# Buffers of split weights kept as the last weight ring, and a rearranged router start, in a one-core hybrid decoder step

## The chip, the cores and the metric

The kernel runs on one core of a Trainium2 chip. The metric is the time of one execution on the device, in microseconds; lower is better. Times of the kernel before are the median of 3 runs. TensorE is called PE here, VectorE DVE, ScalarE ACT, GpSimd POOL; SP is the engine that issues most of the DMA transfers.

## What is computed

One layer of a decoder for 256 prompt tokens and 32 sample tokens (8 sequences of 4), 288 tokens in all, with a model width of 1024, in fp32:

```python
xn = rms_norm(x)
q_sb, k_sb, v_sb, q_m, k_m, v_m, gate_sb, gate_m = split(xn @ w_in)       # 1024 x 5120
m = sigmoid(gate_sb) * (stick_breaking(q_sb, k_sb, v_sb) @ w_proj_sb) \
  + sigmoid(gate_m) * (block_attention(q_m, k_m, v_m) @ w_proj_moba)
x = x + m @ w_out
x = x + hier_moe(rms_norm(x))    # best of 4 groups, then 2 of its 4 experts; 16 SwiGLU experts of 256
y = rms_norm(x) * g_final
```

The sample tokens also attend to 256 past keys each, which are gathered from paged pools. Outputs are y and the new keys and values. On the inputs used, the 288 tokens choose 576 experts; 234 of these choices fall on experts 10 to 15, and no expert has more than 64 tokens.

## The kernel before, in words

Activations lie transposed, features on partitions, tokens along the free axis. The work goes through these stages.

**Projections and attention (0 to 217 us).** `w_in` is loaded in chunks of 256 columns (1 MB, tag `raw`, three buffers). Each group of 128 columns (`g1`) is split into a high part h (a cast on ACT, L355) and a low part l (a subtraction on DVE, L360), and `held` (L374, L375, L378) makes three products of it: 16 matmuls that use h, then 8 that use l. h and l have three buffers each (tags `wh` and `wl` of the pool `wp`). Attention runs between those groups. The order on PE is set by a hand-written driver; on ACT and DVE a scheduler sets it from its own model of the program.

**Output projections (217 to 274 us).** `proj` and `outp` do the same with `w_proj` and `w_out`; the last three groups, o5, o6 and o7, hold the last three buffers of h and l. The router's logits (`lgp`) are accumulated beside them.

**Router (274 to 289 us).** ACT and DVE follow the written order from here. `natural` turns x back to token rows, `rows_out` stores them to `x2_d` in DRAM. DVE finds groups and experts and makes one-hot tables; PE counts the places in each expert (`cums`), then makes, for the 8 pairs of experts, the list of tokens of each slot (`index_mm`: token numbers times one-hot, L995; `index` adds the parts on DVE). A pair has 128 slots. Pair 0 does not use its list: its rows are selected by a product with the one-hot table (`pick`, L1013, in two halves of 512 columns, the copies out of PSUM on ACT for half 0 and on DVE for half 1, L1014). Its norm factors come from another such product (L1053 into `pi`, copied to `rsl` by L1063). `turn_xe` (L1022) then transposes the rows and scales them (L1024). `warm` (L201) is a matmul of ones whose result nobody reads; one stands before `cums`, one behind. Pairs 1 to 7 are gathered from `x2_d` by an indirect DMA on POOL's queue (`fetch`, L1004), which leaves out slots whose index is past the end.

**Experts (289 to 397 us).** `up` (L1185) multiplies a pair with gate and up weights, `down` (L1233) with the down weights. In the middle of pair 0, `late_router` counts again for an overflow check (L1081) and makes the other lists. Results of pairs 0 to 4 are stored as rows to `y_d` (L1244), and six indirect DMAs (`gathered`, L1282) later fetch two rows for each token; `rows2` holds the row numbers and `add_rows` (L1291) adds the rows with the weights `w2`. A choice that falls on a late expert (10 to 15, pairs 5 to 7, added by products instead) points to one of 16 rows of zeros behind the others, written by L917.

**The weight ring.** The 48 MB of expert weights come as 48 parts of 1 MB (two DMAs for gate and up, one for down), in order of use. They rotate through 19 slots that are set up as memory comes free: `RINGS = (8, 5, 3, 3)`. The third group are the `raw` buffers. The fourth are three slots of a new pool, `ring3`, allocated after `wp` has been released. SP issues the parts in order; a part waits until all products that used its slot are done. Parts are counted from 0 here: parts 16, 17 and 18 are the first of the fourth group, and part 19 is the first that takes a slot already used, that of part 0, which pair 0 has read when four of its eight steps k are done.

```python
    ring_loads(RINGS[2])                 # L896: parts 13 to 15, right after the last outp
    gx.release()
    wp.release()
    for c in range(2):                   # L927
        for t in range(c == 0, 3):
            natural(t, c)
        if c:
            ring_loads(1)                # part 16
        last = rows_out(slice(c * 512, c * 516 + 512))
    with tc.issue_after(last.ins):
        ring_loads(RINGS[3] - 1)         # parts 17 and 18
```

Of the kernel before, what the change touches and what calls it, by code (L numbers as in the profile page):

```python
# [7 lines left out]
F32 = mybir.dt.float32  # L8
# [111 lines left out]
def build(tc, I, O):  # L120
# [17 lines left out]
    x2_d = dr.tile([NT, D + 4], F32, name="x2_d")  # L138
    y_d = dr.tile([NONE + 16, D], F32, name="y_d")
    NBUF = {"mm": 2, "at": 4, "ss": 1, "po": 1}  # L140
# [64 lines left out]
    def startup():  # L205
# [51 lines left out]

        hl = [[wp.tile([128, 8, 128], F32R, tag=f"w{c}", name=f"{c}i{4 + j}") for c in "hl"] for j in range(2)]

# [80 lines left out]

    splits, first = {}, []

# [10 lines left out]
    def split_h(src, name, shape=(8, 128)):  # L353
        h = wp.tile([128, *shape], F32R, tag="wh", name=f"h{name}")
        nc.scalar.copy(h, src)  # L355
        return h

    def split_l(src, h, name, shape=(8, 128)):
        l = wp.tile([128, *shape], F32R, tag="wl", name=f"l{name}")
        V.tensor_sub(l, src, h.bitcast(F32))  # L360
        return l
# [533 lines left out]
    drv.run()  # L895
    ring_loads(RINGS[2])  # L896
    gx.release()
    wp.release()


    wk = tc.alloc_tile_pool(name="wk", bufs=1)
    rings.append(tc.alloc_tile_pool(name="ring3", bufs=RINGS[3], side="right"))
    mo = tc.alloc_tile_pool(name="mo", bufs=1)
# [11 lines left out]
    for i in range(2):  # L915
        nc.gpsimd.memset(xes[i], 0.0)
    nc.gpsimd.dma_start(y_d[NONE:, :], xes[0][0:16, 0:D])  # L917
    ioi = mo.tile([128, 384], I32, tag="PT", name="ioi", bufs=2)
# [8 lines left out]
    for c in range(2):  # L927
        for t in range(c == 0, 3):
            natural(t, c)
        if c:  # L930
            ring_loads(1)
        last = rows_out(slice(c * 512, c * 516 + 512))
    with tc.issue_after(last.ins):
        ring_loads(RINGS[3] - 1)
    for t in range(3):
# [23 lines left out]

    warm(1, 416)  # L960
    cums = P("mm", "cums")
# [47 lines left out]
    def pick(c):  # L1009
        po = P("at", f"xe0{c}")  # L1010
        cs = slice(c * 512, c * 512 + 512)
        for t in range(3):
            mm(po, slots_of(t, 0), x2[:TW[t], t, cs], start=(t == 0), stop=(t == 2))  # L1013
        (nc.scalar.copy, V.tensor_copy)[c](xe0[:, cs], po)  # L1014

# [35 lines left out]
    V.tensor_tensor(ee, ee, bc(s4[:, :, None], 2), op=ALU.mult)  # L1051
    for t in range(3):
        mm(pi[:, 16:17], slots_of(t, 0), x2[:TW[t], t, D:D + 1], start=(t == 0), stop=(t == 2))  # L1053
    xe0 = gt.tile([128, 4 * NT], F32, tag="xT", name="xe0")
    pick(0)
    index_mm(0, 3)
    index(0, 3)
    fetch(1)
    fetch(2)
    pick(1)  # L1060
    xeTs[0] = gt.tile([128, 4 * NT], F32, tag="xT", name="xeT0")[:, 0:D].rearrange("p (k t) -> p k t", k=8)
    rsl[0] = mo.tile([128, 1], F32, tag="rsl", name="rsl0", bufs=3)
    V.tensor_copy(rsl[0], pi[:, 16:17])  # L1063
    turn_xe(xeTs[0], xe0, 0)
    V.tensor_reduce(es, ee, axis=AX.X, op=ALU.add)
# [13 lines left out]
    def late_router():  # L1079
        for t in range(3):  # L1080
            mm(cums[:, 48:64], onesb[:TW[t], :], OHs[:TW[t], t, :], start=(t == 0), stop=(t == 2))  # L1081
        index_mm(3, 8)
        index(3, 8)
        V.tensor_reduce(mxc, cums[:, 48:64], axis=AX.X, op=ALU.max)
        V.tensor_copy(mxi, mxc)
        V.tensor_scalar(tmp, posm, float(CAP) + 0.5, None, op0=ALU.is_ge)
        V.tensor_mul(cw, cw, tmp)
        token_rows()
        hold.__exit__(None, None, None)

    def token_rows():

        pk, row, ok = s3("pk", 2), s3("row", 2), s3("ok", 2)
        for i in range(2):
            V.tensor_mul(tmp, posm, OH[i])
            V.tensor_reduce(pk[:, :, i], tmp, axis=AX.X, op=ALU.add)
        V.scalar_tensor_tensor(row, ei[:, :, 0:2], float(CAP), pk, op0=ALU.mult, op1=ALU.add)
        V.tensor_scalar(ok, pk, CAP + 0.5, None, op0=ALU.is_lt)
        V.scalar_tensor_tensor(ok, ei[:, :, 0:2], 2 * LATE - 0.5, ok, op0=ALU.is_lt, op1=ALU.mult)
        V.scalar_tensor_tensor(row, row, -(NONE + 1.0), ok, op0=ALU.add, op1=ALU.mult)  # L1100
        V.tensor_scalar(rows2, row, float(NONE), None, op0=ALU.add)

# [172 lines left out]
    def gathered():  # L1275

        last.append(tc.manual_schedule(engines={mybir.EngineType.Activation, mybir.EngineType.DVE}))
        last[0].__enter__()
        g = [ring_slot(48 + t, f"yg{t}") for t in range(3)]
        for t in (1, 0, 2):  # L1280
            for i in range(2):
                nc.gpsimd.indirect_dma_start(out=g[t][:TW[t], i * D:(i + 1) * D], out_offset=None, in_=y_d[:, :],  # L1282
                                             in_offset=bass.IndirectOffsetOnAxis(ap=rows2[:TW[t], t, i:i + 1], axis=0),
                                             bounds_check=NONE + 15, oob_is_err=False)
        yg.extend(g)
        yield 0.0, 0.0
# [111 lines left out]
```

## Time and profile before

| | |
|---|---|
| median of 3 runs | 411.39 us (411.09 to 413.56) |
| profiled execution | 411.19 us |
| its span, first to last instruction | 409.3 us |
| PE busy | 391.2 us (96%) |
| DVE, ACT, POOL busy | 205.5, 182.9, 92.8 us |
| DMA | 111.04 MB, mean 271 GB/s |
| mean granted TensorE clock | 0.995 |

A timeline row gives start, length, engine, line, operation, output and inputs, shape and count; a bracket at its end is the idle time of the engine before it and what ended it. The end of a matmul is modelled, so a row's length runs over the start of the next; here the distance of two starts is used for what an instruction costs on PE. SPq is SP's DMA queue. "x_d" is `x2_d`, "xe" on L1013 is the picked rows, "inv" is `pi`, "gu" is the result of `up` and "pd" that of `down`.

### The profile page before, as it was taken

Reading aid. Unit: us, or ns where it says so; the run is one execution under the profiler, and the core shown is the slowest. Engines: PE = TensorE matmul, PEld = TensorE weight load, DVE = VectorE, ACT = ScalarE, POOL = GpSimd, SP = SyncE. Lnnn points to the kernel's source line nnn. Section 1 sums busy time; section 2 is a strip of 40 time slices with the busy share of each in tenths; the row PEclk is TensorE's granted clock in tenths of the full one; section 3 lists DMA queues with packets and bytes.
Section 4 is the critical chain, followed back from the end, with each engine's and each line's share of the span. In section 5 each row is a group of like instructions: output and inputs, shape, how many; then the busy total and the mean of one; then the engine's idle time right before and its main releaser. Section 6 shows DMA issues by size and latency. Waiting matters only on the chain.

```text
span 409.3 us, 7097 instructions
## 1 busy us (share of the span) xinstructions
PE 391.2 (96%) x2690; PEld 293.0 (72%) x2690; DVE 205.5 (50%) x436; ACT 182.9 (45%) x361; POOL 92.8 (23%) x128
## 2 busy tenths in 40 slices
PE   7999999998999999999999999999899999999990
PEld 4999988867987987897999999994443333333350
DVE  3784468556633647133646794324640111126874
ACT  4864357667753665665544445223001111112353
POOL 2540221204352330510100142330102222023011
PEclk9999999999999999999999999999999999999997
DMA  8999736736733973673699999929799999999903
GB/s 260 320 335 295 234 106 219 236 104 217 260 111 106 336 281 104 205 258 104 168 371 412 325 356 364 420 95 286 254 306 417 409 412 423 414 417 410 353 24 123
DMA packets 56969, 111.04 MB, mean 271 GB/s; under 512 B 7653, under 2 KB 36845, under 8 KB 54881
## 3 DMA queue, kind: packets, MB, share of 16 engines
q1 hardware_dynamic: 49648, 86.55, 59.1%
q0 software_dynamic: 7120, 23.95, 16.1%
q8 instruction: 23, 0.38, 0.4%
q14 instruction: 18, 0.14, 0.1%
q10 hardware_dynamic: 160, 0.03, 0.0%
HBM read 104.64 MB, written 7.43 MB: 274 GB/s over the span
## 4 chain that ended last, share of the span: by engine, by line
PE 71%; DMA 18%; DVE 4%; ACT 2%; issue 2%; POOL 0%; DVEq 0%; SPq 0%; POOLq 0%; ACTq 0%
DMA w<-in_w_expert_up 15%; PE g L378 9%; PE g L374 9%; PE g L375 9%; DMA w<-in_w_expert_down 4%; PE gu L1185 4%; PE pk L643 3%; PE p L374 2%; PE p L375 2%; PE p L378 2%; PE ss L649 2%; PE pos L674 2%; PE pd L1233 2%; PE g L302 2%; PE o L374 2%
## 5 line engine op out<-in xcount | busy, mean ns | idle before, releaser
L374 PE MATMUL g<-xTh,hi 128*128 128x288 f32 x304 | 88.4, 311 | 0.0
L375 PE MATMUL g<-xTl,hi 128*128 128x288 f32 x304 | 83.3, 296 | 0.0
L1185 PE MATMUL gu<-w,xeT 128*64 128x512 f32 x256 | 60.3, 598 | 0.8 <-DMA w<-in_w_expert_up 0.5
L374 PEld LDWEIGHTS g<-xTh,hi 128*128 128x128 f32 x304 | 57.2, 188 | 0.9 <-issue 0.7
L375 PEld LDWEIGHTS g<-xTl,hi 128*128 128x128 f32 x304 | 57.4, 189 | 0.0
L378 PE MATMUL g<-xTh,li 128*128 128x288 f32 x304 | 49.3, 300 | 0.0
L360 DVE TENSOR_TENSOR li<-rawi,hi 128x1024 fp32r<-128x1024 f32 x38 | 46.1, 1215 | 4.7 <-ACT hi L355 4.7
L355 ACT CAST hi<-rawi 128x1024 fp32r<-128x1024 f32 x38 | 39.7, 1048 | 15.6 <-PE g L375 15.4
L378 PEld LDWEIGHTS g<-xTh,li 128*128 128x128 f32 x304 | 42.8, 189 | 1.7 <-issue 1.7
L1185 PEld LDWEIGHTS gu<-w,xeT 128*64 128x64 f32 x256 | 18.1, 136 | 31.8 <-issue 29.7
L1233 PE MATMUL pd<-w,hT 128*64 128x512 f32 x128 | 29.2, 598 | 0.0
L1024 DVE TENSOR_TENSOR xeT<-xe,gpk 128x512 f32<-128x512 f32 x16 | 10.4, 686 | 22.9 <-PE xe L1022 22.9
L532 DVE TENSOR_TENSOR gate<-g,rb 128x288 f32<-128x288 f32 x16 | 7.3, 456 | 28.7 <-PE g L378 28.7
L644 ACT COPY KT<-pk 128x512 f32<-128x512 f32 x29 | 18.0, 642 | 7.2 <-PE pk L643 6.7
L1203 DVE SCALAR_TENSOR_TENSOR h<-gu,rsl,h 128x256 f32<-128x256 f32 x8 | 3.9, 484 | 34.4 <-ACT h L1200 34.3
L1200 ACT ACTIVATE h<-gu,rsl 128x256 f32<-128x256 f32 x8 | 3.8, 474 | 35.9 <-PE gu L1185 19.8
L1004 POOL DMA_INDIRECT xe<-x_d,inv x7 | 7.3, 1037 | 55.0 <-DVE rsl L1172 26.2
L1233 PEld LDWEIGHTS pd<-w,hT 128*64 128x64 f32 x128 | 8.6, 136 | 15.4 <-issue 13.7
L643 PE MATMUL pk<-blob,kp 128*128 128x128 f32 x128 | 19.4, 274 | 0.1
L374 PE MATMUL p<-oTh,hp 128*128 128x288 f32 x64 | 17.5, 296 | 0.0
L375 PE MATMUL p<-oTl,hp 128*128 128x288 f32 x64 | 17.4, 294 | 0.0
L1243 ACT COPY y<-pd 128x512 f32<-128x512 f32 x10 | 5.9, 586 | 23.6 <-PE pd L1233 23.6
(306 smaller groups left out, 719.3 us busy)
## 6 DMA issues: line engine op xcount, KB each, us to landing
rawi<-in_w_in SPq DMA_DIRECT2D x19, 1024.0 KB
w<-in_w_expert_gate SPq DMA_DIRECT2D x32, 512.0 KB
w<-in_w_expert_up SPq DMA_DIRECT2D x32, 512.0 KB
w<-in_w_expert_down SPq DMA_DIRECT2D x16, 1024.0 KB
rawo<-in_w_out SPq DMA_DIRECT2D x4, 1024.0 KB
y_d<-y POOLq DMA_DIRECT2D x10, 256.0 KB
rawp<-in_w_proj_sb SPq DMA_DIRECT2D x2, 1024.0 KB
rawp<-in_w_proj_moba SPq DMA_DIRECT2D x2, 1024.0 KB
```

What stands on the lines that cost most here:

```text
L302: mm(o[j], hl[j][a][:, k, :], b[:, k, :], start=(k == 0 and a == 0 and b is xTh), stop=(k == 7 and a == 1))
L355: nc.scalar.copy(h, src)
L360: V.tensor_sub(l, src, h.bitcast(F32))
L374: mm(o, h[:, k, :], mh[k], start=(k == 0), stop=False)
L375: mm(o, h[:, k, :], ml[k], start=False, stop=False)
L378: mm(o, l[:, k, :], mh[k], start=False, stop=(k == n - 1))
L643: nc.tensor.transpose(pv[:, j, :], kp[:, c, j * 128:(j + 1) * 128], ident)
L644: nc.any.tensor_copy(kt[:, :, c:256:2], pv)
L649: mm(pt[32 * bb:32 * bb + 32, 0:260], Qb[:, j, 4 * G + bb, :, :].rearrange("p h q -> p (h q)"), KT[bb][:, j, :], start=(j == 0), stop=(j = ...
L1024: i = V.tensor_mul(xeT[:, ks, :], pv, gpk[:, ks, None].broadcast_to([128, 4, 128]))
L1185: mm(pt[64 * i:64 * i + 64, :], xeTs[pr][:, k, 64 * i:64 * i + 64], W[pr, k // 4, i][:, :, k % 4, :], start=(k == 0), stop=(k == 7))
L1233: mm(pd[64 * i:64 * i + 64, :], hT[:, k, 64 * i:64 * i + 64], W[pr, 2, i][:, k, c * 512:(c + 1) * 512], start=(k == 0), stop=(k == 1))
```

## The change

- **Split weights.** h and l of a group now are the two halves of one tile (tag `w`, 8 KB a partition, three buffers), so both come free together, after the last product with l. The same memory as before.
- **Last ring.** The pool of these tiles is not released; it is the fourth group of the ring. Parts 16 to 18 are issued right behind 13 to 15, each when its buffer comes free, ahead of the row stores.
- **Rows of late experts.** The zero rows and their store are gone. Such choices get a row number past the end, which the gather leaves out; their weight in `w2` is set to 0 by one more DVE multiplication.
- **Router.** The first `warm` is two matmuls instead of one. Pair 0 has no list made. Its norm product stands behind the second half of `pick` rather than ahead of the first. The copy of the second half is shared by ACT and DVE, 256 columns each. The count for the overflow check stands right ahead of pair 0's `up` rather than inside it, and the copy to `rsl` stands behind `turn_xe`.

```diff
-    y_d = dr.tile([NONE + 16, D], F32, name="y_d")
+    y_d = dr.tile([NONE, D], F32, name="y_d")
...
     def split_h(src, name, shape=(8, 128)):
-        h = wp.tile([128, *shape], F32R, tag="wh", name=f"h{name}")
+        hl = wp.tile([128, 2, *shape], F32R, tag="w", name=f"hl{name}")
+        h = hl[:, 0]
+        lows[name] = hl[:, 1]
...
     def split_l(src, h, name, shape=(8, 128)):
-        l = wp.tile([128, *shape], F32R, tag="wl", name=f"l{name}")
+        l = lows.pop(name)
...
-    ring_loads(RINGS[2])
+    rings.append(wp)
+    ring_loads(RINGS[2] + RINGS[3])
     gx.release()
-    wp.release()
...
-    rings.append(tc.alloc_tile_pool(name="ring3", bufs=RINGS[3], side="right"))
...
-    nc.gpsimd.dma_start(y_d[NONE:, :], xes[0][0:16, 0:D])
...
-        if c:
-            ring_loads(1)
-        last = rows_out(slice(c * 512, c * 516 + 512))
-    with tc.issue_after(last.ins):
-        ring_loads(RINGS[3] - 1)
+        rows_out(slice(c * 512, c * 516 + 512))
...
-    warm(1, 416)
+    warm(2, 416)
...
-        (nc.scalar.copy, V.tensor_copy)[c](xe0[:, cs], po)
+        if c == 0:
+            nc.scalar.copy(xe0[:, cs], po)
+        else:
+            nc.scalar.copy(xe0[:, 512:768], po[:, 0:256])
+            V.tensor_copy(xe0[:, 768:1024], po[:, 256:512])
...
-    for t in range(3):
-        mm(pi[:, 16:17], slots_of(t, 0), x2[:TW[t], t, D:D + 1], start=(t == 0), stop=(t == 2))
...
-    index_mm(0, 3)
-    index(0, 3)
+    index_mm(1, 3)
+    index(1, 3)
...
     pick(1)
+    for t in range(3):
+        mm(pi[:, 16:17], slots_of(t, 0), x2[:TW[t], t, D:D + 1], start=(t == 0), stop=(t == 2))
...
+    turn_xe(xeTs[0], xe0, 0)
     V.tensor_copy(rsl[0], pi[:, 16:17])
-    turn_xe(xeTs[0], xe0, 0)
+    for t in range(3):
+        mm(cums[:, 48:64], onesb[:TW[t], :], OHs[:TW[t], t, :], start=(t == 0), stop=(t == 2))
...
     def late_router():
-        for t in range(3):
-            mm(cums[:, 48:64], onesb[:TW[t], :], OHs[:TW[t], t, :], start=(t == 0), stop=(t == 2))
...
-        V.scalar_tensor_tensor(row, row, -(NONE + 1.0), ok, op0=ALU.add, op1=ALU.mult)
-        V.tensor_scalar(rows2, row, float(NONE), None, op0=ALU.add)
+        V.scalar_tensor_tensor(row, row, -(BIG + 1.0), ok, op0=ALU.add, op1=ALU.mult)
+        V.tensor_scalar(rows2, row, float(BIG), None, op0=ALU.add)
+        V.tensor_mul(w2, w2, ok)
...
-                                             bounds_check=NONE + 15, oob_is_err=False)
+                                             bounds_check=NONE - 1, oob_is_err=False)
```

How PE's instructions stand between the two fillers' place and pair 0's first expert product. Before, from the second filler on (the first rows of the list for pairs 1 and 2 stand for the rest of it):

```order
L201 MATMUL warm<-rst_101 128x416
L1053 MATMUL inv<-x_2665,oh_3476 128x1 x3
L1013 MATMUL xe_3519<-x_2665,oh_3476 128x512 x3
L995 MATMUL inv<-blob,oh_3476 128x2 x3
L995 LDWEIGHTS oneh_3477
L995 MATMUL inv<-tokb,oneh_3477 128x2
...
L1013 MATMUL xe_3542<-x_2665,oh_3476 128x512 x3
L1022 MATMUL xe_3550<-blob,xe_3518 128x128 x4
L1022 MATMUL xe_3556<-blob,xe_3518 128x128 x4
L1185 MATMUL gu_3577<-w_2714,xeT_3547 64x512
```

The same place in the changed kernel:

```order
L201 MATMUL warm<-rst_101 128x416
L1012 MATMUL xe_3456<-x_2625,oh_3416 128x512 x3
L994 LDWEIGHTS oneh_3417
L994 MATMUL inv<-tokb,oneh_3417 128x2
...
L1012 MATMUL xe_3476<-x_2625,oh_3416 128x512 x3
L1063 MATMUL inv<-x_2625,oh_3416 128x1 x3
L1025 MATMUL xe_3487<-blob,xe_3455 128x128 x4
L1025 MATMUL xe_3493<-blob,xe_3455 128x128 x4
L1069 LDWEIGHTS onesb
L1069 MATMUL cums<-OHs,onesb 128x16
...
L1189 MATMUL gu_3518<-w_2674,xeT_3485 64x512
```

The norm product moved behind the picks, the three matmuls of pair 0's list are gone, and the count moved up to the place ahead of the first expert product.

How SP's transfers stand around the row stores (w is a part of the expert weights, x_d the stored rows). Before, parts 15 to 19:

```order
L881 DMA w_3363<-in_w_expert_gate 128x1024
L881 DMA w_3363<-in_w_expert_up 128x1024
L881 DMA w_3427<-in_w_expert_gate 128x1024
L881 DMA w_3427<-in_w_expert_up 128x1024
L816 DMA x_d<-x_2665 128x2x512
L817 DMA x_d<-x_2665 32x512
L816 DMA x_d<-x_2665 128x2x516
L817 DMA x_d<-x_2665 32x516
L881 DMA w_3432<-in_w_expert_gate 128x1024
L881 DMA w_3432<-in_w_expert_up 128x1024
L881 DMA w_3435<-in_w_expert_down 128x2048
L881 DMA w_3662<-in_w_expert_down 128x2048
```

In the changed kernel, parts 16 to 19:

```order
L886 DMA w_3310<-in_w_expert_gate 128x1024
L886 DMA w_3310<-in_w_expert_up 128x1024
L886 DMA w_3313<-in_w_expert_gate 128x1024
L886 DMA w_3313<-in_w_expert_up 128x1024
L886 DMA w_3316<-in_w_expert_down 128x2048
L821 DMA x_d<-x_2625 128x2x512
L822 DMA x_d<-x_2625 32x512
L821 DMA x_d<-x_2625 128x2x516
L822 DMA x_d<-x_2625 32x516
L886 DMA w_3601<-in_w_expert_down 128x2048
```

Parts 17 and 18 moved ahead of the row stores; part 19 still follows them.

How ACT's instructions stand around one cast in the attention stage. Before:

```order
L541 ACTIVATE t_1203<-t_1203 128x384
L542 ACTIVATE t_1194<-t_1194 128x384
L355 CAST hi_1391<-rawi_1389 128x1024
L542 ACTIVATE t_1203<-t_1203 128x384
L687 COPY oT_113<-pd_1245 64x4x16 x2
L644 COPY KT_1257<-pk_1259 128x4x128
L472 COPY nr_1269<-ntr_1265 128x384
```

In the changed kernel:

```order
L546 ACTIVATE t_1185<-t_1185 128x384
L547 ACTIVATE t_1176<-t_1176 128x384
L547 ACTIVATE t_1185<-t_1185 128x384
L360 CAST hli_1371<-rawi_1369 128x1024
L692 COPY oT_113<-pd_1226 64x4x16
L649 COPY KT_1238<-pk_1240 128x4x128
L692 COPY oT_113<-pd_1226 64x4x16
L477 COPY nr_1250<-ntr_1246 128x384
```

The scheduler put the cast one place later, and a copy of attention's keys between two others; some fifteen more casts of these stages moved by a place or two in the same way, and subtractions on DVE with them.

## Rows read from the trace of the kernel before

**Rows 1.** The page: the chain that ended last, by engine and by line.

```profile
PE 71%; DMA 18%; DVE 4%; ACT 2%; issue 2%; POOL 0%; DVEq 0%; SPq 0%; POOLq 0%; ACTq 0%
DMA w<-in_w_expert_up 15%; PE g L378 9%; PE g L374 9%; PE g L375 9%; DMA w<-in_w_expert_down 4%; PE gu L1185 4%; PE pk L643 3%; PE p L374 2%; PE p L375 2%; PE p L378 2%; PE ss L649 2%; PE pos L674 2%; PE pd L1233 2%; PE g L302 2%; PE o L374 2%
```

**Rows 2.** Busy time by stretch; last columns: granted clock, DMA share, GB/s.

```profile
268.00:274.00 6.00, 6.00 (x52) 5.89 (x50) 1.57 (x3) 0.89 (x2) 2.92 (x4) 1.00 0.05 18
...
280.00:292.00 12.00, 10.79 (x44) 5.27 (x45) 5.61 (x25) 2.33 (x5) 2.06 (x2) 1.00 0.94 307
...
310.00:385.00 75.00, 74.81 (x354) 27.36 (x350) 20.78 (x38) 13.70 (x26) 14.07 (x18) 1.00 1.02 408
```

**Rows 3.** Timeline of PE in the expert stage: one pair after another, and the end.

```profile
308.87 6.18 PE L1185 MATMUL gu<-w,xeT 128*64 128x512 f32 x28
...
321.01 6.18 PE L1185 MATMUL gu<-w,xeT 128*64 128x512 f32 x28
...
385.67 3.62 PE L1185 MATMUL gu<-w,xeT 128*64 128x512 f32 x14 [0.46 <-DMA w<-in_w_expert_up]
```

**Rows 4.** Timeline of SP's queue, 274 to 282 us: parts 16, 18 and 19.

```profile
274.22 0.33 SPq L881 DMA_DIRECT2D w<-in_w_expert_gate  x1
...
281.19 12.29 SPq L881 DMA_DIRECT2D w<-in_w_expert_down  x2
```

**Rows 5.** Timeline of PE in the router, 276 to 294 us.

```profile
276.33 0.86 PE L201 MATMUL warm<-rst 128*128 128x416 f32 x2
277.96 0.17 PE L967 MATMUL cums<-OHs,trib 128*128 128x16 bf16 x1 [0.77 <-DVE OHs L957]
...
279.08 0.81 PE L1053 MATMUL inv<-x,oh 128*128 128x1 f32 x6
279.81 3.03 PE L1013 MATMUL xe<-x,oh 128*128 128x512 f32 x6
282.78 0.92 PE L995 MATMUL inv<-blob,oh 128*128 128x2 f32 x6
283.63 0.55 PE L995 MATMUL inv<-tokb,oneh 128*128 128x2 bf16 x6
284.10 3.04 PE L1013 MATMUL xe<-x,oh 128*128 128x512 f32 x6
288.01 1.14 PE L1022 MATMUL xe<-blob,xe 128*128 128x128 f32 x8 [0.88 <-DVE rsl L1063]
289.48 4.58 PE L1185 MATMUL gu<-w,xeT 128*64 128x512 f32 x20 [0.33 <-DVE xeT L1024]
293.99 0.32 PE L1081 MATMUL cums<-OHs,onesb 128*128 128x16 bf16 x3
```

**Rows 6.** Timeline of DVE at 287 us: the copy of the second half.

```profile
287.17 0.69 DVE L1014 COPY xe<-xe 128x512 f32<-128x512 f32 x1 [2.54 <-PE xe L1013]
```

**Rows 7.** Timeline at 392 us: an ACT copy of 256 columns out of PSUM.

```profile
391.67 0.37 ACT L1217 COPY hT<-ph 128x256 f32<-128x256 f32 x1 [0.56 <-PE ph L1215]
```

**Rows 8.** DMA queues (packets, MB, share) and issues with KB each.

```profile
q0 software_dynamic: 7120, 23.95, 16.1%
...
y_d<-y POOLq DMA_DIRECT2D x10, 256.0 KB
...
kp<-in_cache_sb_k,pidx POOLq DMA_INDIRECT x8
```

**Rows 9.** PE's waits, 0 to 276 us: first and last of six (total, times, longest).

```profile
PE warm L201 <- POOL rst L178: 2.9, 1, 2.9
...
PE sc L579 <- ACT nr L472: 0.2, 1, 0.2
```

**Rows 10.** All engines' waits, 0 to 276 us: the casts.

```profile
ACT hi L355 <- PE g L375: 15.4, 17, 2.2
```

**Rows 11.** The chain in order of time: products with l of o5 and of o7.

```profile
263.03 1.07 PE o L378 x8
...
270.74 1.07 PE o L378 x8
```

More of the change, by code (lines that the diff above doesn't have):

```diff
@@ L256, in low @@
             eng.tensor_sub(xTl[:, ks, cols], xgt[i % 3][:, ks, 0:n], xTh[:, ks, cols].bitcast(F32))
-        hl = [[wp.tile([128, 8, 128], F32R, tag=f"w{c}", name=f"{c}i{4 + j}") for c in "hl"] for j in range(2)]
+        hl = []
+        for j in range(2):
+            t = wp.tile([128, 2, 8, 128], F32R, tag="w", name=f"hli{4 + j}")
+            hl.append((t[:, 0], t[:, 1]))
         def part(j, hf, low_):
@@ L338, in startup @@
         return pidx
-    splits, first = {}, []
+    splits, lows, first = {}, {}, []
     def raw(key, src, shape=(8, 256)):
```

## The prediction

> **What bounds the kernel now.** I read the chain first. It gives PE 71% and DMA 18%, and its costliest line is the loading of expert weights, 15% [rows 1]. Taken alone, that says: load more, earlier. The busy time by stretch seems to agree. From 310 to 385 us the DMA share is 1.02 at 408 GB/s, while from 268 to 274 us it is 0.05 [rows 2]. That gap is a place where weights could move and don't.
>
> The timeline of PE corrects this. Pair 1's expert products start at 308.87 us and pair 2's at 321.01, 12.14 us later, and no row there has a wait in it [rows 3]. Over 310 to 385 us PE is busy 74.81 of 75 us at a granted clock of 1.00 [rows 2]. The only wait on a weight is 0.46 us, at 385.67 us [rows 3]. So the stream runs level with PE: the chain names it because the very last wait lies there, yet PE sets the pace, and faster weights alone give back 0.46 us. What counts is when PE starts on pair 0 (289.48 us, [rows 5]), and what it does from then on.
>
> The place where PE doesn't work is the router. Between 280 and 292 us it is busy 10.79 of 12 us [rows 2], and some of its work there is done one product behind the other though something could lie beside a copy [rows 5]. Before 276 us PE waits six times, from 2.9 us at the very start down to 0.2 us [rows 9].
>
> **The change part by part.** The sum is made against the profiled execution, 411.19 us (span 409.3 and 1.9 around it); the median shown is 0.20 above that.
>
> *Router, up to pair 0's first product.* By the distance of starts [rows 5]:
> - The norm product leaves its place ahead of the first half: 279.81 - 279.08 = 0.73 us earlier.
> - Pair 0's list is gone: 283.63 - 282.78 = 0.84 us. (Pairs 1 and 2 stay, 0.47 us.)
> - The second half's product takes 2.97 us (as the first, 282.78 - 279.81), so it ended about 287.07 and the transposes began at 288.01: 0.94 us, in which DVE copied for 0.69 us [rows 6]. ACT copies 256 columns in 0.37 us [rows 7], so two half copies are done some 0.5 us behind the product. The norm product lies beside them now and takes 0.73 us, so it ends last: I take 0.73 in place of 0.94, a gain of 0.21. Bounds: nothing, if a half copy is no shorter, and 0.45, if the products overlap.
> - The second filler. The first began at 276.33 and PE waited 0.77 us for DVE's table until 277.96. One filler takes 0.81 us (the other one, 278.27 to 279.08, [rows 5]; its start isn't shown but stands 0.10 behind the last count, so I use 0.8 to 0.86). Two end at about 278.0, against 277.96. I take a loss of 0.05; bounds 0 and 0.15. The granted clock is 1.00 in every stretch shown [rows 2], which is the 2.4 GHz level, so the filler has nothing to give back.
>
> Together 0.73 + 0.84 + 0.21 - 0.05 = 1.73 us. What DVE makes for these products is ready in time: `rsl` is copied later but first used after pair 0.
>
> *The count (L1081).* It took 294.25 - 293.99, some 0.26 us, inside pair 0. It now fills the 0.33 us in which PE waited for the scaled rows [rows 5]. Gain 0.26; if it doesn't fit, nothing.
>
> *Last ring.* Three parts are loaded as o5, o6 and o7 are done, which is from 264.1 to 271.8 us [rows 11], instead of 274 to 292 us [rows 4]. They fall into the empty stretch, and the row stores behind them on SP are issued no later, since they came at 275 us, behind part 16 of 274.22. But part 19 needs slot 0, which pair 0 frees after four steps: SP held it until 293 us (the second of the two issues of 12.29 us, [rows 4]). All 19 slots are then full by 276 us and the stream stands still until pair 0 has begun. So 3 MB / 408 GB/s = 7.7 us of loading move out of 280 to 292 us, and the stream's next part moves only with PE, by 1.73 us. Gain by itself: 0; between 0 and 0.46.
>
> *Rows of late experts.* 234 of 576 rows of 4 KB are not read: 0.96 MB, 2.35 us of the stream at 408 GB/s. That skipped rows move nothing is in the queue's total: 32 page gathers of 0.52 MB (8 issues in each of four groups) and 10 stores of 0.26 MB make 19.4 of 23.95 MB [rows 8]; 2.4 MB are the present row gathers, and 2.1 are left for 7 fetches, which would be 3.7 if empty slots moved. With the stream 2.35 us shorter and as early as PE, the wait of 0.46 us goes. After it the products of pair 7 and the final norm come as before: nothing else is late there. Gain 0.46, between 0 and 0.46. The extra DVE multiplication lies in pair 0, beside PE.
>
> *Split weights in one buffer.* A cast now waits for the group's last product with l, 1.07 us after its last with h [rows 11], and the scheduler moved it by a place or two. PE needs a group's h two groups after its buffer comes free, more than 5 us later in the dense stages, for a cast and a subtraction of 2.3 us: hidden there. In attention ACT's order matters. The copy that PE waits for at one such place now stands one place further back, behind another copy; at others attention's own work moved ahead of the cast. The waits to be won are 5.9 - 2.9 = 3.0 us (the six of [rows 9] without the start's). Bounds: a gain of 2, a loss of 5 (below); I take 0, since the casts move both ways round the same waits.
>
> **Sum:** -1.73 - 0.26 - 0.46 = -2.45 us, 408.7 us against the profiled execution, 408.9 against the median.
>
> **The skill against the row.** PE is busy 74.81 of 75 us in the expert stage, but its weight loads only 27.36 [rows 2]. The Trainium skill, "Perfetto Trace Analysis", section "Identifying the Most-Contended Engine", says that matmul busy time is a poor measure of how near PE is to its roof, and that the busy share of weight loads is better. By that rule PE has room here and the weights bind. That is the second rival below; the equal distance of 12.14 us without waits speaks against it.
>
> **The rivals.**
> 1. *The weights bind, and all the loading moved counts.* Then 7.7 + 2.35 us go: 401.1 us. For it: the chain [rows 1]. Against it: part 19's wait for pair 0, and a PE without waits [rows 3].
> 2. *The weights bind, but restart with PE.* Then the end moves with the restart and the shorter stream, 1.73 + 2.35 = 4.1: 407.1 us. For it: DMA share 1.02. Against it: one wait of 0.46 us in 75.
> 3. *The router's gain does not reach the end,* because the last weights land when they did: only what lies behind them could move, 411 us. Against it: the stream's restart hangs on pair 0.
> 4. *Slower: casts held longer stall ACT.* ACT already waits 17 times for a buffer of h, 15.4 us in all [rows 10], and each such wait can grow by 1.07 us [rows 11], with softmax steps queued behind it and PE behind those. All 17 would be 18 us. From the third that reaches PE the change loses (2.45 us are used up); with five it is 411.2 - 2.45 + 5.35 = 414.1 us. More than 1% needs seven. For it: the order on ACT and DVE did change. Against it: the scheduler knew of the shared buffer and placed casts later.
>
> **How the numbers follow.** Forecast 0.62; rival 1 0.06, rival 2 0.08, rival 3 0.10, rival 4 0.14. The forecast's own range is 407.5 to 410.3, by the bounds of the router's terms and about a microsecond from attention. The range to hold 8 in 10 takes in rival 3 and the top of rival 2: 406.9 to 412.0. About 1%, 4.1 us, is what a measurement of this kernel can tell from no change. Below 407.3 lie rival 1, half of rival 2 and a little of the forecast: 0.15. Above 415.5 lies the upper third of rival 4: 0.05. The rest, 0.80, is within 1%.
>
> **What would show it.** Right: pair 0's first product 11.4 us after the first filler's start instead of 13.15 (289.48 - 276.33); parts 16 to 18 issued at about 264, 268 and 272 us; DMA near still between 278 and 291; the distance of 12.14 us kept; no wait at pair 7; 0.96 MB less on the POOL queue. Wrong: a shorter distance between pairs (rival 1 or 2), a wait on weights at the end as long as the router's gain (rival 3), or a first filler that starts later than 276.33 (rival 4).

## The result, and the profile after

The changed kernel took 409.46 us in the median (408.44 to 411.46, 15 executions), the kernel before 411.64 beside it (410.38 to 415.39, 15). The ratio is 0.9935, with a 95% interval of 0.9911 to 0.9959. The forecast was 408.9 us, within 406.9 and 412.0. The profiled execution took 409.46 us, its span is 407.7. One thing is needed to read the numbers below: every execution is recorded with PE's mean granted clock, the long executions of the kernel before are mostly those with a low one, and ratios and counts leave out executions more than 1.5% above the fastest of their kernel.

Three lines of the page of after: POOL's DMA queue, the chain by engine, and the casts. They answer to [rows 8], [rows 1] and, over the whole span, [rows 10]:

```profile
q0 software_dynamic: 7088, 22.93, 15.8%
...
PE 69%; DMA 18%; DVE 5%; ACT 4%; issue 2%; POOL 0%; DVEq 0%; SPq 0%; POOLq 0%; ACTq 0%
...
L360 ACT CAST hli<-rawi 128x1024 fp32r<-128x1024 f32 x38 | 39.7, 1048 | 25.8 <-PE g L383 25.3
```

ACT has gained 2 points in the chain, although it does no more work: it now holds others up. The queue of POOL moved 1.02 MB less than in [rows 8]: the forecast's 0.96 and the 0.07 of the zero rows that are no longer stored.

Busy time by stretch, in the columns of [rows 2]:

```profile
268.00:274.00 6.00, 6.00 (x51) 5.94 (x50) 1.58 (x3) 0.89 (x2) 0.80 (x1) 1.00 1.01 380
280.00:292.00 12.00, 11.73 (x51) 5.81 (x52) 6.82 (x29) 2.70 (x6) 2.04 (x2) 1.00 0.27 77
310.00:385.00 75.00, 74.54 (x354) 27.40 (x352) 22.45 (x40) 14.54 (x28) 13.54 (x17) 1.00 1.02 407
```

The DMA gap has moved from 268 to 274 us (now 380 GB/s) into 280 to 292 us (now 77). PE's stretch in the router is fuller, 11.73 of 12 us instead of 10.79.

SP's queue shows why. Part 16 goes out 9.4 us earlier than in [rows 4] and part 18 8.7, but part 19 at 292.30 still waits for pair 0:

```profile
264.84 0.33 SPq L886 DMA_DIRECT2D w<-in_w_expert_gate  x1
...
268.68 0.33 SPq L886 DMA_DIRECT2D w<-in_w_expert_gate  x1
...
272.54 0.33 SPq L886 DMA_DIRECT2D w<-in_w_expert_down  x1
...
292.30 0.34 SPq L886 DMA_DIRECT2D w<-in_w_expert_down  x1
```

The timeline of PE in the router, against [rows 5], and two pairs of the expert stage and the end, against [rows 3]:

```profile
277.02 1.56 PE L201 MATMUL warm<-rst 128*128 128x416 f32 x4
278.65 0.17 PE L966 MATMUL cums<-OHs,trib 128*128 128x16 bf16 x1
...
279.77 2.99 PE L1012 MATMUL xe<-x,oh 128*128 128x512 f32 x6
282.69 0.55 PE L994 MATMUL inv<-tokb,oneh 128*128 128x2 bf16 x6
283.17 3.04 PE L1012 MATMUL xe<-x,oh 128*128 128x512 f32 x6
286.13 0.91 PE L1063 MATMUL inv<-x,oh 128*128 128x1 f32 x6
287.12 1.16 PE L1025 MATMUL xe<-blob,xe 128*128 128x128 f32 x8
288.12 0.31 PE L1069 MATMUL cums<-OHs,onesb 128*128 128x16 bf16 x3
288.62 4.58 PE L1189 MATMUL gu<-w,xeT 128*64 128x512 f32 x20 [0.19 <-DVE xeT L1027]
...
307.76 6.18 PE L1189 MATMUL gu<-w,xeT 128*64 128x512 f32 x28
...
319.89 6.18 PE L1189 MATMUL gu<-w,xeT 128*64 128x512 f32 x28
...
384.36 1.94 PE L1189 MATMUL gu<-w,xeT 128*64 128x512 f32 x8 [0.26 <-DMA w<-in_w_expert_up]
```

From the first filler to pair 0's first product it is 11.60 us instead of 13.15, and the pairs keep their distance (319.89 - 307.76 = 12.13). So far the forecast. But the first filler itself starts at 277.02, later than the 276.33 of before: the sign that the forecast named for rival 4.

**Where the time went.** I matched PE's products of after with those of before, in order, and took the difference of their starts, called PE's offset below. It is -1.61 us at 13 us, +0.69 at 274, -1.11 in the expert stage and -1.31 at 395 us. So after won 1.61 us at the start, lost 2.30 in attention and the dense stages, won 1.80 in the router and 0.20 at the end. The 1.61 is no work of the change. PE's transposes of x at the start, of before and then of after:

```profile
6.16 4.99 PE L243 MATMUL xt<-blob,xs 128*128 128x128 f32 x24
```

```profile
6.16 3.50 PE L243 MATMUL xt<-blob,xs 128*128 128x128 f32 x24
```

In the clock's records of the trace of before, the first stretch at full rate begins only 12.47 us into the span; in that of after at 7.54. (Where there is no record, the views by stretch print 1.00; the longer products show the lower rate.) Among the 14 traces of this study, of all kernels, it was 12.3 to 12.5 in three and 5.8 to 8.2 in the rest, the unchanged kernel among both. Without it the trace of after is some 0.3 us behind before, while the median is 2.2 ahead. The experiments had to find both: what costs 2.3 us, and what gives back more.

### The profile page after: what moved, and what is told of

Same layout as the page of the kernel before. It is cut to its first block, busy times and chain, and to the rows that moved or that the text cites. A ratio compares the mean times of both kernels' runs of the same rounds, so it can differ in the third digit from the quotient of the medians.

```text
span 407.7 us, 7087 instructions
## 1 busy us (share of the span) xinstructions
PE 389.5 (96%) x2686; PEld 290.5 (71%) x2686; DVE 206.4 (51%) x435; ACT 183.2 (45%) x364; POOL 90.5 (22%) x127
## 4 chain that ended last, share of the span: by engine, by line
PE 69%; DMA 18%; DVE 5%; ACT 4%; issue 2%; POOL 0%; DVEq 0%; SPq 0%; POOLq 0%; ACTq 0%
DMA w<-in_w_expert_up 15%; PE g L383 9%; PE g L379 9%; PE g L380 9%; DMA w<-in_w_expert_down 4%; PE gu L1189 4%; PE pk L648 3%; PE p L379 2%; PE p L380 2%; PE p L383 2%; PE ss L654 2%; PE pos L679 2%; PE pd L1237 2%; PE o L379 2%; PE sc L584 2%; PE po L620 2%
## 5 line engine op out<-in xcount | busy, mean ns | idle before, releaser
L379 PE MATMUL g<-xTh,hli 128*128 128x288 f32 x304 | 88.3, 311 | 0.0
L380 PE MATMUL g<-xTl,hli 128*128 128x288 f32 x304 | 83.3, 296 | 0.0
L379 PEld LDWEIGHTS g<-xTh,hli 128*128 128x128 f32 x304 | 57.2, 188 | 0.9 <-issue 0.7
L380 PEld LDWEIGHTS g<-xTl,hli 128*128 128x128 f32 x304 | 57.4, 189 | 0.0
L365 DVE TENSOR_TENSOR hli<-rawi,hli 128x1024 fp32r<-128x1024 f32 x38 | 46.4, 1222 | 17.8 <-ACT hli L360 17.1
L360 ACT CAST hli<-rawi 128x1024 fp32r<-128x1024 f32 x38 | 39.7, 1048 | 25.8 <-PE g L383 25.3
L383 PE MATMUL g<-xTh,hli 128*128 128x288 f32 x304 | 49.4, 300 | 0.0
L383 PEld LDWEIGHTS g<-xTh,hli 128*128 128x128 f32 x304 | 42.9, 189 | 1.7 <-issue 1.7
L1237 PEld LDWEIGHTS pd<-w,hT 128*64 128x64 f32 x128 | 8.6, 136 | 15.4 <-issue 13.7
L379 PE MATMUL p<-oTh,hlp 128*128 128x288 f32 x64 | 17.5, 297 | 0.0
L380 PE MATMUL p<-oTl,hlp 128*128 128x288 f32 x64 | 17.4, 294 | 0.0
```

What stands on the lines that cost most here:

```text
L379: mm(o, h[:, k, :], mh[k], start=(k == 0), stop=False)
L380: mm(o, h[:, k, :], ml[k], start=False, stop=False)
L383: mm(o, l[:, k, :], mh[k], start=False, stop=(k == n - 1))
L1237: mm(pd[64 * i:64 * i + 64, :], hT[:, k, 64 * i:64 * i + 64], W[pr, 2, i][:, k, c * 512:(c + 1) * 512], start=(k == 0), stop=(k == 1))
```

## Experiments

Every run stood beside runs of the kernel before on its chip. Their medians were 413.27 us for the first four kernels, 410.77 for the next four and 412.22 for the last four (29 to 35 executions each). The kernels themselves ran 12 times each, the first and the one with one filler 6 times.

**Shared buffers or not.** The first kernel is the change without the shared buffers and the early ring (edits against the changed kernel, cut):

```diff
-        hl = wp.tile([128, 2, *shape], F32R, tag="w", name=f"hl{name}")
...
+        h = wp.tile([128, *shape], F32R, tag="wh", name=f"h{name}")
...
-    rings.append(wp)
-    ring_loads(RINGS[2] + RINGS[3])
+    ring_loads(RINGS[2])
...
```

> The kernel before with the router's and the row gather's edits; h and l keep buffers of their own and parts 16 to 18 are loaded late, as before. Theory A (the prediction's: the router gives 2.0 us, the shorter stream up to 0.46, the shared buffers and the early ring nothing): 409.2 us where before is 411.6, ratio 0.994, the same as the changed kernel. Theory B (the shared buffers cost about 2.3 us in attention, as the start of the first filler against the end of PE's warm-up in the two traces suggests): 2 us or more faster than the changed kernel, ratio to before 0.994 and of the changed kernel 0.999. The trace should show the count of groups between PE's warm-up and the first filler as long as before under both, pair 0's first product 11.6 us behind the first filler, and the wait at pair 7 not above 0.5 us.

Measured: 407.93 us (407.17 to 409.43), ratio 0.9889 (0.9841 to 0.9937): faster than either theory had. The second has only these two parts, in the kernel before:

> The kernel before with shared buffers for h and l and with parts 16 to 18 loaded as these come free; router and gather as before. Theory A: no change, 411.6 us, ratio 1.000 (0.998 to 1.001), with the empty stretch of the stream moved from 268 to 274 us to 280 to 292 us. Theory B: slower by about 2.3 us, ratio 1.005, all of it before the first filler. A third theory, that early weights are what made the changed kernel faster: 409.3 us, ratio 0.994.

Measured: 414.27 us (411.54 to 417.73), ratio 1.004 (1.0005 to 1.0075). The changed kernel again, as measure for both:

> The changed kernel once more, for its times beside the others on this chip and a second trace. Ratio to before 0.9935 again. If the start of PE's full rate (12.5 us into the span in the trace before, 7.5 in the one after) is chance, the 1.6 us that lie there show up differently in this trace; if it is the change's doing, 7.5 us again. The stretch from there to the first filler should again be about 2.3 us longer than before.

Measured: 410.56 us, ratio 0.9942 (0.9909 to 0.9975): 2.6 us above the first. Between 13 and 274 us the offset of PE against before's trace is -0.12 us with separate buffers, +2.73 and +2.97 in the two kernels with shared ones. So these two parts together take back about half of the 5.3 us that the rest of the change brings there.

**More relief for the weights.** The changed kernel, where pair 7 uses the weights of pair 6, so 6 MB are not loaded (pair 7's own weights are left out of the computation):

> The changed kernel, but pair 7 multiplies with pair 6's weights, so 6 MB of loads at the end are left out (its results for experts 14 and 15 are those of 12 and 13). If PE sets the pace: only the last wait of 0.26 us goes, 409.2 us where the changed kernel has 409.5, ratio between the two 0.999. If the weights set it: 6 MB at 408 GB/s are 15 us, of which at least 4 should show, 405.5 us or less, and the distance between two pairs falls under 12.14 us.

Measured: 409.34 us, ratio 0.9921 (0.9888 to 0.9954), 1.2 us under the changed kernel beside it. The timelines of PE at pair 7's last products, with the weights loaded, then without that:

```profile
383.73 4.56 PE L1189 MATMUL gu<-w,xeT 128*64 128x512 f32 x16
```

```profile
383.20 3.60 PE L1192 MATMUL gu<-w,xeT 128*64 128x512 f32 x16
```

The sixteen products take 0.96 us less, without a wait being marked in either, and 0.5 us more are won at 372 us; up to there the pairs keep their distance, 12.14 us. So the loads bind at the very end alone, for 1.2 us by the median and 1.5 by PE's offset at 395 us.

**The filler.** The first kernel of this section with one filler, then the kernel before with two (`warm(1, 416)` against `warm(2, 416)`, nothing else):

> The kernel of e1_no_ring with one filler ahead of the counts instead of two, nothing else changed. Theory A (the filler has nothing to give back): the same as e1_no_ring, 407.9 us, and the same spread. Theory C (e2_ring_only's trace shows the granted clock halved for 3.4 us behind the router's waits; the second filler keeps PE busy there and prevents it in most executions): some executions 1.5 to 3 us longer, median 409 to 411 us, and a trace with a half-rate stretch near the second half of pick if the profiled execution is one of them.

> The kernel before with two fillers ahead of the counts instead of one, nothing else changed. Theory A: 0.05 us slower than before in its trace and no difference in the median, ratio 1.000. Theory C: the executions at 413 to 416 us become rarer, median 410 to 411.5 us where before has 413.3 on this chip, ratio 0.993 to 0.997. If the waits behind the pick (0.9 us) halve the clock too, little changes.

Measured: 406.16 us (405.6 to 407.36), ratio 0.9878 (0.9831 to 0.9925), and 410.13 us, ratio 1.0002 (0.9969 to 1.0036). By their ratios both are what theory A said. The second filler is worth nothing by itself, and the change without it loses nothing, as far as these intervals tell.

**The early ring alone.** Here h and l stay apart, and only the last groups, those of w_out, share buffers, in a pool of their own that becomes the last ring:

```diff
-    rings.append(tc.alloc_tile_pool(name="ring3", bufs=RINGS[3], side="right"))
+    rings.append(wq[0])
```

> e1_no_ring, but the groups of w_out, and these alone, put h and l in one tile of a pool that becomes the last ring: parts 16 to 18 are loaded early without any shared buffer in the attention stage. Theory B (sharing costs in attention, early parts give nothing): the same as e1_no_ring, 407.5 to 408.3 us, PE's progress from its warm-up to the first filler as before. If early parts are worth something by themselves: below 407 us. If shared buffers cost in the output projections too: above 409 us.

Measured: 408.32 us (407.05 to 410.47), ratio 0.995 (0.9928 to 0.9972). PE's waits from 0 to 276 us show a new one, for the casts into the new pool:

```profile
PE o L796 <- ACT hlo L359: 1.1, 1, 1.1
...
PE o L796 <- DVE hlo L364: 0.2, 1, 0.2
```

There, at 241 us, PE's offset loses 2.1 us. So this kernel can't price the ring by its time, but its end can: from 384 to 395 us it wins 0.33 us on before, the one-filler kernel with its late ring 0.32. The early ring changes nothing where it should pay, as far as two traces can tell: there the unchanged kernel's own two differ by 0.62 us.

**The kernel before as a kernel of its own,** for another trace:

> The kernel before, for a second trace and its times beside the others. If the late start of PE's full rate in the first trace (12.5 us into the span, against 6.5 to 8.2 in five other kernels' traces) is chance, it starts at 6.5 to 8.2 us here and the first filler stands 1.4 us earlier, at about 274.9 us. Theory C: among its executions some are 2 to 5 us longer than the shortest, which is at 409.7 to 410.

Measured: 409.79 us, ratio 0.996 (0.9926 to 0.9993), from 407.82 to 416.99: this much two sets of the same kernel differ. Its trace reaches full rate at 7.69 us and is 1.54 us ahead of the first one at 13 us, like after. Up to the router it then wins another 0.96 us, which was not expected: at 99.7 us PE waits 1.42 us in the first trace and not at all in this one. That wait is missing in all four traces of this set, and in all others PE waits there 1.4 us or more, so offsets from 13 to 274 us carry about a microsecond that has nothing to do with the edits.

**Which edit takes the long executions away.** The router's edits in two halves. First the list and the norm product (with it the copy to `rsl` moves behind `turn_xe`, as in the change):

```diff
-    for t in range(3):
-        mm(pi[:, 16:17], slots_of(t, 0), ...)
     pick(0)
-    index_mm(0, 3)
+    index_mm(1, 3)
...
     pick(1)
+    for t in range(3):
+        mm(pi[:, 16:17], slots_of(t, 0), ...)
...
+    turn_xe(xeTs[0], xe0, 0)
     V.tensor_copy(rsl[0], pi[:, 16:17])
-    turn_xe(xeTs[0], xe0, 0)
```

> The kernel before with two of the router's edits: pair 0's list of rows dropped, and the norm product moved behind the second half of the gather product. By the prediction's terms: 0.84 + 0.73 = 1.57 us earlier at pair 0, the copies as before (the norm product now lies beside DVE's copy, so up to 0.2 more). Theory A (each edit is worth its own term, and the long executions of before have nothing to do with these two): median 1.6 to 1.8 us under before, and the spread of before stays (8 us, with executions 3 to 5 us above the median). Theory B (the long executions of before, 3 to 4 us above the others, arise at these two small products): they go, so that all executions lie within 3 us of each other and the median falls by 3 to 5 us. Rival C (a gain at pair 0 doesn't reach the end): no change in the median.

Measured: 409.41 us (408.12 to 412.45), ratio 0.9937 (0.9902 to 0.9972). PE's timeline in its router:

```profile
279.05 2.99 PE L1013 MATMUL xe<-x,oh 128*128 128x512 f32 x6
281.97 0.55 PE L995 MATMUL inv<-tokb,oneh 128*128 128x2 bf16 x6
282.45 3.03 PE L1013 MATMUL xe<-x,oh 128*128 128x512 f32 x6
285.42 0.91 PE L1060 MATMUL inv<-x,oh 128*128 128x1 f32 x6
286.36 1.13 PE L1022 MATMUL xe<-blob,xe 128*128 128x128 f32 x8
```

The gain in the router is 1.64 us by PE's offset. The median falls by more, 2.8, a little less than theory B's 3 to 5, and the executions span 4.3 us instead of 3. Then the split copy and the count:

> The kernel before with the other two edits: the second half's copy split between ACT and DVE, and the count of slots moved ahead of pair 0. Theory A: no norm product lies beside the copies here, so PE waits only some 0.3 to 0.4 us less for them, and the count gives 0.26: median 0.3 to 0.7 us under before, spread as before. Theory B (long executions arise at the list and the norm product): the same 0.3 to 0.7 with the spread of before. Rival D (they arise at the wait for the copy or at the count): spread within 3 us, median 2 to 4 us lower.

Measured: 413.11 us (409.57 to 415.17), ratio 1.0026 (0.9993 to 1.006); by PE's offset 0.18 us are won in the router. The count wins 0.25, and up to pair 0's first product 0.08 are lost: the split copy brings none of the 0.3 to 0.4 us expected. Seven of the 12 executions have a mean clock below 0.987, as theory B has it. And the rows of late experts alone:

> The kernel before with the rows of late experts not gathered, and nothing else: 1.0 MB less on the POOL queue. Theory A: only the last wait on weights (0.46 us in the trace of before) can shrink, so the median is 0 to 0.5 us under before and the spread stays. Rival E (the long executions of before are those in which the weights arrive late at the end, and the shorter stream takes them away): spread within 3 us and a median 2 us lower.

Measured: 410.8 us (408.13 to 412.96), ratio 0.9987 (0.9954 to 1.002). In its trace 0.77 us are won at pair 7, none before; but the unchanged kernel's second trace wins 0.62 there too, so the trace alone doesn't price the edit. Last, the shared buffers without the ring:

> The kernel before with h and l of each weight group in one shared buffer, and nothing else (the last ring is loaded late, as before). Theory A (the shared buffers cost 2.3 to 2.9 us in attention, whatever the ring does): median 2 to 3 us above before, about 1.006; PE's offset against before grows by 2.3 to 2.9 us between 12 us and the router. Rival F (the loss belongs to the pool of split buffers becoming the last ring): no change against before, offset within 0.3 us.

Measured: 414.14 us (412.09 to 416.81), ratio 1.0051 (1.0018 to 1.0085). PE's offset grows by 4.56 us from 13 to 274 us, 1.56 of it in a stretch at half rate. So the loss belongs to the buffers, and rival F falls. This trace also shows what lowers the mean clock; neither trace of the kernel before caught one of its long executions. Busy time by stretch, the granted clock third from the end:

```profile
98.00:101.00 3.00, 1.16 (x10) 1.10 (x10) 3.00 (x5) 2.09 (x5) 0.16 (x1) 1.00 0.98 313
101.00:105.00 4.00, 4.00 (x22) 3.98 (x22) 2.02 (x7) 0.99 (x2) 1.00 (x1) 0.57 0.49 124
288.00:292.00 4.00, 2.96 (x12) 1.27 (x10) 1.34 (x3) 0.00 (x0) 2.06 (x2) 1.00 0.96 343
292.00:296.00 4.00, 3.83 (x10) 1.78 (x12) 3.86 (x13) 0.00 (x0) 0.00 (x0) 0.57 0.51 190
```

From 101.34 us, and again from 292.49, the clock stands at half, 1.2 GHz, for 3.41 us. PE loses 1.56 us of offset to the first and 1.69 to the second. Ahead of the first PE waited 1.84 us, of the second 0.88 us for the copies and 0.33 for the scaled rows. The Trainium skill, "TensorE: Matmul & The Clock Gate", section "HAM oscillation — how this bites in real kernels", tells of such falls behind waits for DMA. The trace agrees that PE idled ahead of each, but both waits in the router are short and for DVE. They are not needed either: in the trace of the kernel with shared buffers and early ring the clock falls at 286.39 us, inside the second half's product, ahead of both, and PE's last wait, of 0.84 us, lies 6.8 us back. The norm product and the list are among what stands in between.

## Why the prediction was right, and where it was not

| kernel | buffers | PE's offset won (-) or lost (+): 13 to 274 us | 276 to 309 us | 384 to 395 us | median |
|---|---|---|---|---|---|
| changed | shared | +2.30 | -1.80 | -0.20 | 409.46 |
| changed, again | shared | +2.73 | -1.81 | -0.55 | 410.56 |
| without shared buffers and ring | apart | -0.12 | -1.81 | -0.12 | 407.93 |
| the same, one filler | apart | -0.89 | -1.82 | -0.32 | 406.16 |
| list and norm alone | apart | +0.05 | -1.64 | +0.03 | 409.41 |
| copy and count alone | apart | +0.07 | -0.18 | +0.36 | 413.11 |
| rows alone | apart | +0.14 | -0.01 | -0.77 | 410.80 |
| two fillers alone | apart | -1.02 | 0.00 | +0.18 | 410.13 |
| shared buffers alone | shared | +4.56, half rate 1.56 of it | +1.70, all half rate | -0.48 | 414.14 |
| before, again | apart | -0.96 | -0.02 | -0.62 | 409.79 |

The medians stand beside four different sets of runs of before, so they are compared by the ratios above, not down the column.

The time was right to 0.6 us, and that is luck: a loss of 2.3 to 3.0 us that the forecast put at nothing was made up by a gain from the clock, about 1.5 us, that it didn't have, and by rows that are worth more than its 0.46.

- **Router and count: right.** Forecast -1.73 and -0.26, together -1.99; measured together -1.80 to -1.82 in the six traces with all of the edits (in one without the filler). To pair 0's first product it is -1.55, the count adds -0.25. Alone, the norm product gave 0.74 and the list 0.89, where I had 0.73 and 0.84. What is missing is the split copy. The filler cost nothing: 1.63 us from its start to the table's products, with one and with two.
- **The split copy: the bound of nothing.** I gave it and the norm product beside it 0.21. DVE's half starts when ACT's is done. Of after, both engines at 286 us:

```profile
286.24 0.37 ACT L1016 COPY xe<-xe 128x256 f32<-128x256 f32 x1 [2.75 <-PE xe L1012]
286.64 0.42 DVE L1017 COPY xe<-xe 128x256 f32<-128x256 f32 x1 [2.95 <-ACT xe L1016]
```

  One behind the other they take 0.37 + 0.42 us; the single copy took 0.69 [rows 6]. From the second half's product to the transposes it is 3.95 us (287.12 - 283.17), against 3.91 before. The order stands in the program: DVE's half waits for the semaphore that ACT's half raises, where the whole copy of before waits for PE's. Whether the two could run side by side without it was not tried.
- **Last ring: right.** Worth 0 as far as the runs tell, since part 19 waits for pair 0.
- **Rival 2 (the weights bind): at the very end alone.** The Trainium skill's rule on weight loads ("Perfetto Trace Analysis", "Identifying the Most-Contended Engine") would have given PE room there; with 6 MB less to load the pairs kept their 12.14 us up to 372 us, and 1.2 to 1.5 us came off behind that.
- **Rows of late experts: put too small, place open.** I said 0.46 at most and no wait at pair 7; it is 0.26 us in this trace. Alone, the edit moved the median by -1.4 us with an interval that includes no change. At equal mean clock (the fit below) its executions are 1.3 us shorter than before's, within 0.6. No trace shows where.
- **Split weights in one buffer: wrong.** This is the step that failed: "I take 0, since the casts move both ways round the same waits." They cost 2.3 to 3.0 us (half-rate stretches aside), within my bound of 5 and as rival 4 has it. Measured from 20 us on, behind the start, the five traces lie at 2.3 to 2.6; against the second trace of before it is 1.3 more. ACT's waits for a buffer were 15.4 us, 17 times [rows 10]. ACT's and PE's waits in the trace of after, 0 to 276 us:

```profile
ACT hli L360 <- PE g L383: 25.3, 21, 2.2
```

```profile
PE ntr L446 <- ACT KT L649: 2.4, 2, 1.7
PE rt L491 <- ACT t L613: 1.6, 1, 1.6
```

  The largest step in PE's offset, 0.94 us in every trace with shared buffers, is the wait of 1.60 us, which was 0.66 before. The timeline of before at that place:

```profile
83.91 1.05 ACT L355 CAST hi<-rawi 128x1024 fp32r<-128x1024 f32 x1
...
86.12 0.87 ACT L540 ACTIVATE t<-sc 128x384 f32<-128x384 f32 x2 [0.36 <-PE sc L582]
...
87.30 0.48 ACT L608 COPY t<-pa 128x384 f32<-128x384 f32 x1
...
87.83 0.55 PE L486 MATMUL rt<-blob,nr 128*128 128x128 f32 x3 [0.66 <-ACT t L608]
```

  And that of after:

```profile
84.56 0.51 PE L383 MATMUL g<-xTh,hli 128*128 128x288 f32 x2
84.68 0.87 ACT L545 ACTIVATE t<-sc 128x384 f32<-128x384 f32 x2 [0.36 <-PE sc L587]
...
85.43 1.05 ACT L360 CAST hli<-rawi 128x1024 fp32r<-128x1024 f32 x1
...
86.79 0.48 ACT L613 COPY t<-pa 128x384 f32<-128x384 f32 x1
...
87.33 0.55 PE L491 MATMUL rt<-blob,nr 128*128 128x128 f32 x3 [1.60 <-ACT t L613]
```

  In before the cast fills time in which ACT has nothing else. In after its buffer comes free later, with the last products with l at 84.56, and the scheduler put the cast behind the first softmax step, ahead of the copies that PE waits for. A cast of 1.05 us in such a place is nearly all PE's loss there (0.94). The other 1.4 us come in steps of 0.2 to 0.45 (at 100, 148, 178 and 246 us among others), which were not followed to a cast each. The place that I saw in the order is another, at 97 us: there the cast itself waits 0.83 us for its buffer and PE 1.70 us, against the 1.42 of before's first trace. I let moves at other places balance it; they don't, since PE waits for few of ACT's steps, and a cast that leaves idle time costs only where it lands.
- **What I did not have: the long executions.** I wrote that the clock of 1.00 leaves the filler nothing to give back. That held for the filler. But one trace at full clock doesn't show the executions that lose it. Of those compared, 48 of 155 with before's list and norm product had a mean clock below 0.987 (before: 31 of 96; its list and norm product with other edits: 17 of 59). With the list dropped and the norm product moved it was 0 of 75, in six kernels. Below 0.990 it is 81 of 155 against 5 of 75, so moving the two makes falls rare but doesn't end them. In the set of the first four kernels the mean clock of before is 0.9867, of the changed kernel 0.9921, and before's executions get 2.76 us longer with every 0.01 of clock: 1.5 of the 2.3 us by which their means differ.

So by the traces and the clock the change is two gains, the router's 1.8 us and the clock's 1.5, less a loss of 2.3 to 3.0 for the buffers. That leaves -0.3 to -1.0 us; the 2.2 to 2.7 measured are more. The recorded times close the sum. A least-squares fit over the 191 compared executions of the three sets of experiments, without the kernel with 6 MB less and the one with the early ring alone, has a level for each set, a term for each edit and one for the mean clock. It gives list and norm -1.5 us, copy and count nothing (-0.05), rows -1.4, shared buffers with or without the early ring +2.1, each within 0.4, and 2.8 us for every 0.01 of clock. The edits add up to -0.8 us; with the clock's 1.5 that is -2.3, as the means differ. The fit takes the effects to add and the clock to act by its mean; it is no experiment of its own. Which of the small products in the router lets the clock fall was not separated: list, norm product and the copy to `rsl` were moved together.

The version without shared buffers and early ring beats both kernels: 407.93 us beside 410.56 for the changed kernel in the same set. With one filler it has 406.16 us, ratio 0.9878 (0.9831 to 0.9925).

## What to carry to other kernels

Two buffers merged into one hold the longer of two lifetimes; don't balance the moved casts against each other, but look, place by place, at what now stands ahead of the one step that the bounding engine waits for. Small products on PE can cost more than their own length where the clock falls behind them, and a single trace at full clock doesn't show it: look at the clock of all executions. A copy divided over two engines is a gain only if the trace shows the halves side by side.

## What the runs showed of the hardware

- PE's clock came up at 5.8 to 8.2 us or at 12.3 to 12.5 us into the span, in the same kernel too (7.69 and 12.47); by 20 us this moved a trace by 0.8 to 1.6 us. Offsets between two single traces are read from behind that point.
- The clock fell to half for stretches of 3.41 us each, with no wait longer than 0.9 us in the router ahead of it; in the trace with two of them they cost 1.56 and 1.69 us.
- An unchanged kernel's two traces differed by 3.1 us of PE's offset at 395 us: 1.2 at the start, 1.3 at one wait in attention, 0.6 at the last pair.
